# A hybrid encoder step on one core: side work timed by a model of engines and buffers instead of fixed waits

## The chip, the cores and the metric

The kernel runs on one core of a Trainium2 chip. The metric is the device time of one execution in microseconds (us); the median of three runs counts. The engines of the core are TensorE (PE: matmuls and transposes), VectorE (DVE), ScalarE (ACT), GpSimd (POOL) and SyncE (SP), which here issues the DMAs. Each has its own queue of instructions and works through it in order.

## The reference, cut to what matters

One step of a one-layer encoder over a prompt of 2048 tokens and a sample of 32, in float32, width 1024:

```python
h = rms_norm(x, norm1);  z = h @ w_in            # w_in: 1024 x 3592
qa, fa, ia, ga, qb, kb, vb, fb = split(z)
# HGRN2: 4 heads, chunks of 64 tokens, state 128 x 128 per head
f = lb + (1 - lb) * sigmoid(fa)
S_t = diag(f_t) S_{t-1} + outer(1 - f_t, ia_t);   o_t = S_t^T qa_t
oa = rms_norm(o, hgrn_out_norm) * silu(ga)
# FoX: 8 heads of 64; q and k normalized per head; c = cumsum(log_sigmoid(fb + b))
s = q @ k.T / 8 + c_q - c_k        # causal
ob = softmax(s) @ v
x = x + concat(oa, ob) @ w_out
y = x + square(relu(rms_norm(x, norm2) @ w_up)) @ w_down      # 1024 -> 4096 -> 1024
```

Normalized keys, values, the log forget values and the final states are outputs as well. The sample goes through the same weights and attends to a cache of 256 rows.

## The kernel before

The tokens are taken in four blocks of 512; block 2 carries the 32 sample tokens too (544 columns). All large products run in float32r as three matmuls: a value is split into a high part and a remainder, and `mm3` adds high by high, high by low and low by high. A strip is one weight tile against one block of tokens: 24 matmuls of 512 columns for 128 output columns and 8 slices of the inner dimension. `load_w` (L158 to L170) brings a weight tile: a DMA of 512 KB into `wr`, a cast on ACT into `wh` (L163) and four subtractions on POOL into `wl` (L169, 256 columns each). `wr`, `wh` and `wl` have two buffers each.

Dense work is these strips: the input projections of FoX (`fox`: for each of four column groups `fox_k`, `fox_v`, `fox_q`, after `fox_gate`) and of HGRN2 (`hgrn`), then `out_proj` and `ffn`. Everything else is side work. After a strip of k or q, `finish` squares the result (`squares`: a product on POOL, L290; a rounded square on ACT, L292; the difference on POOL, L294), sums the squares over a head with two matmuls into a PSUM tile `tk` or `tq`, takes the inverse root on ACT (L282, L283), scales on DVE (L427), stores, and for k transposes on PE (a second `tk`). HGRN2 does the like with `th`. `build` makes the normalized inputs of a block: for each 128 rows a DMA into `row` (L242), two squares on ACT into `junk` (L246), a root on POOL (L156), a scaling on DVE (L251) and eight transposes into two tiles `ta` (L104), each followed by a cast on ACT (L201) and a difference on DVE (L202). `attention` runs head by head over key blocks of 512; `att_max` computes row maxima (`mx`, then transposes into `mt`), `att_main` the scores `st`, the exponentials and, two steps behind, the products with the values (`ot`). Its loads `kA`, `kB`, `V` have two buffers each and are written in the code at the start of the key block that uses them.

The order in which this is emitted is set by the class `Flow` (L42 ff.). `flow.t` is a clock that each matmul advances by a modelled time. `dense` runs the generators of strips and, between matmuls, `pump` runs every side generator whose due time has come. A side generator ends a step with `yield x`: it is due again x microseconds later. These are fixed numbers: QLAT 8.0 from the squares of k and q to their sum, HLAT 7.0 for `th`, KLAT 5.0 to the transposes, BLAT 7.5 in `build`, TLAT 1.2 between the `ta` tiles, SL 4.5 after a strip, PACE for a step of attention. The framework then orders each engine's queue by its own scheduler, with the emission order as its input; the loads in particular are moved far ahead of the place where the code has them.

In time: blocks 0 and 1 of FoX until about 205 us; HGRN2 heads and FoX of blocks 2 and 3, with attention beside them, until about 1015 us; then the pools of temporaries close, the input rows of the residual are loaded (`load_x`, tiles `acc`), and `out_proj` and `ffn` run until the end, with attention beside them until about 2320 us and with `build` for each block's second norm, which reads the residual from `X`.

Of the kernel before, what the change touches and what calls it, by code (L numbers as in the profile page):

```python
# [19 lines left out]
P = 128  # L20
# [20 lines left out]
class Flow:  # L41
# [3 lines left out]
    def __init__(self):  # L45
        self.t = 0.0
        self.n = 0
        self.q = []

    def spawn(self, gen, lat=0.0):  # L50
        self.n += 1
        heapq.heappush(self.q, (self.t + lat, self.n, gen))

    def step(self):
        due, n, gen = heapq.heappop(self.q)
        self.t = max(self.t, due)
        lat = next(gen, None)
        if lat is not None:
            heapq.heappush(self.q, (self.t + lat, n, gen))
# [14 lines left out]

@with_exitstack
def hymba_step(
# [15 lines left out]
    AT = 9  # L92

    def mm(out, lhsT, rhs, start, stop):
        n = rhs.free_size()
        if rhs.dtype == F32:
            flow.t += max(n, 32) * 4 * 0.00042
        else:
            flow.t += n * 0.00042 if n >= 256 else 0.213
        pe.matmul(out, lhsT, rhs, start=start, stop=stop)  # L100

    def tp(out, in_, idn):
        flow.t += 0.109
# [13 lines left out]
    const = ctx.enter_context(tc.tile_pool(name="const", bufs=1))  # L117
    acts = ctx.enter_context(tc.tile_pool(name="acts", bufs=2))
    wpool = ctx.enter_context(tc.tile_pool(name="wpool", bufs=2))
    rows = ctx.enter_context(tc.tile_pool(name="rows", bufs=2))  # L120
    small = ctx.enter_context(tc.tile_pool(name="small", bufs=4))
    att = ctx.enter_context(tc.tile_pool(name="att", bufs=2))
    ps_x = ctx.enter_context(tc.tile_pool(name="ps_x", bufs=3, space=PSUM))
    ps_o = ctx.enter_context(tc.tile_pool(name="ps_o", bufs=1, space=PSUM))
    ps_stack = ExitStack()
    ps_mm = ps_stack.enter_context(tc.tile_pool(name="ps_mm", bufs=2, space=PSUM))
    ps_tr = ps_stack.enter_context(tc.tile_pool(name="ps_tr", bufs=2, space=PSUM))
# [14 lines left out]
    act.preload_act_table_set("natural_log_exp_and_others")  # L142
# [15 lines left out]
    def load_w(src, kt, ncols, pfx):  # L158

        raw = wpool.tile([P, kt, ncols], F32, tag="wraw", name=f"wr{pfx}", bufs=2)  # L160
        sp.dma_start(raw, src.rearrange("(k p) c -> p k c", p=P))
        hi = wpool.tile([P, kt, ncols], F32R, tag="whi", name=f"wh{pfx}")
        act.copy(hi, raw)  # L163
        lo = wpool.tile([P, kt, ncols], F32R, tag="wlo", name=f"wl{pfx}")

        fl = lambda a: a.rearrange("p k c -> p (k c)")
        for c in range(0, kt * ncols, 256):
            s = slice(c, c + 256)
            pool.tensor_tensor(fl(lo)[:, s], fl(raw)[:, s], fl(hi.bitcast(F32))[:, s], op=ALU.subtract)  # L169
# [24 lines left out]
    def to_acts(row, w, hi, lo, t0):  # L194

        for g in range(row.shape[1] // 512):
            tr = ps_tr.tile([P, 4, P], F32, tag="tr", name=f"ta{nid()}")
# [6 lines left out]
            yield TLAT  # L204
# [14 lines left out]
    def build(q, done, gb, getrow, src=None, first=False):  # L219
# [35 lines left out]
        lat = BLAT  # L255
        ts = QT[q]
        cur = prep(*ts[0])
        for i in range(len(ts)):
            nxt = prep(*ts[i + 1]) if i + 1 < len(ts) else None
            yield lat if i == 0 else lat - 3.0  # L260
# [38 lines left out]
    tmp = tmp_stack.enter_context(tc.tile_pool(name="tmp", bufs=12))  # L299
# [4 lines left out]
    def strip(col, A, qs, evac):  # L304
        hi, lo = load_w(w_in[:, col:col + P], KT, P, nid())
        for q in qs:
            ah, al = A[q]
            for c0, n in QCH[q]:
# [5 lines left out]
                if g is not None:  # L314
                    flow.spawn(g, SL)
# [5 lines left out]
    def fox_gate(A, qs):  # L321

# [5 lines left out]
        dve.tensor_tensor(w2[:, :, 32:40], wf, w2.bitcast(F32)[:, :, 0:8], op=ALU.subtract)  # L328
        for q in qs:
# [10 lines left out]
            flow.spawn(gate_tail(q, z), 2.0)  # L340

    def gate_tail(q, z):
# [30 lines left out]
            yield 6.0  # L373
# [18 lines left out]
            if nt == 5:  # L392
                sp.dma_start(nls, X[0:TS, 4, :])
                cg = small.tile([P, 2, HB], F32, tag="cg", name="cg", bufs=1)
                sp.dma_start(cg, cache_logf[0, 0].rearrange("(t p) h -> p t h", p=P))
                st = ps_tr.tile([HB, 512], F32, tag="tr", name=f"tl{nid()}")
# [13 lines left out]
    def fox_k(A, qs, s):  # L410
# [18 lines left out]
        def finish(q, z):  # L429
            n = QN[q]  # L430
            sh, sl = squares(z[:, 0:n])
            yield QLAT
# [7 lines left out]
            if n > 512:  # L440
# [893 lines left out]
    X = {}  # L1334
# [61 lines left out]
```

## Time and profile before

| | us |
|---|---|
| three runs | 2913.29, 2915.94, 2917.99 |
| median | 2915.94 |
| the profiled execution's own time | 2912.88 |
| its span in the trace | 2911.2 |
| PE busy | 2847.8 (98%) |
| DVE, ACT, POOL busy | 1680.2 (58%), 1386.3 (48%), 1278.7 (44%) |
| DMA: bytes moved, mean rate | 381.91 MB, 131 GB/s |

The busy shares are averages over stages. PE is busy nearly everywhere, so what can be gained at the same work is the sum of its gaps, and each gap has a releaser: the instruction on another engine whose end let PE go on. The granted clock of PE is 0.996 of full speed on average.

### The profile page before, as it was taken

The page shows a single profiled execution, that of the slowest core. Times are in us where ns is not written, and L with a number is a line of the kernel's source. Part 1 is how long each engine was busy: PE and PEld are TensorE (multiplying, and loading weights), DVE is VectorE, ACT ScalarE, POOL GpSimd, SP SyncE. Part 2 cuts the span into 40 slices and gives each one's busy share as a digit, 9 for nine tenths or more (in the row PEclk, how much of TensorE's full clock was granted, in tenths as well). Part 3 has the DMA queues.
Part 4 walks back from the last instruction along what each step waited for, and adds up shares of the span by engine and source line. Part 5 has one row for each costly group of instructions (what it writes and reads, how often), then busy time and mean ns, then how long its engine had stood idle before and what let it go on. Part 6 is the DMA issues. An engine that isn't in the chain of part 4 may idle for free.

```text
span 2911.2 us, 43685 instructions
## 1 busy us (share of the span) xinstructions
PE 2847.8 (98%) x15568; PEld 2423.8 (83%) x15568; DVE 1680.2 (58%) x3283; ACT 1386.3 (48%) x2447; POOL 1278.7 (44%) x1744
## 2 busy tenths in 40 slices
PE   7999999999999999999999999999999999999999
PEld 5787877988789778888888888978999989988887
DVE  6336677656666677666565555465665554443333
ACT  5555676777555545444444444444444433222222
POOL 5653344453223444444444444434333454455554
PEclk9999999999999999999999999999999999999999
DMA  6762444776324563434347344444533333243333
GB/s 180 211 170 86 122 137 127 208 193 175 87 80 116 168 227 106 123 107 122 111 123 228 117 120 116 129 134 117 180 113 102 92 109 95 87 131 105 94 94 102
DMA packets 463658, 381.91 MB, mean 131 GB/s; under 512 B 34432, under 2 KB 363408, under 8 KB 463440
## 3 DMA queue, kind: packets, MB, share of 16 engines
q1 hardware_dynamic: 463440, 379.12, 44.9%
q8 instruction: 123, 2.02, 0.3%
q14 instruction: 95, 0.78, 0.1%
HBM read 316.63 MB, written 62.40 MB: 130 GB/s over the span
## 4 chain that ended last, share of the span: by engine, by line
PE 64%; DVE 1%; ACT 0%; DMA 0%; POOL 0%; issue 0%; SPq 0%; DVEq 0%; ACTq 0%; POOLq 0%
PE mm L100 55%; PE st L100 3%; PE ot L100 3%; PE mx L100 1%; PE ta L104 0%; DMA row<-X 0%; PE rs L100 0%; DMA acc<-in_x_prompt_dram 0%; PE tx L104 0%; PE ty L104 0%; POOL wl L169 0%; DVE acc L882 0%; PE mt L104 0%; DVE pl L878 0%; ACT wh L163 0%
## 5 line engine op out<-in xcount | busy, mean ns | idle before, releaser
L169 POOL TENSOR_TENSOR wl<-wr,wh 128x256 fp32r<-128x256 f32 x1536 | 1121.2, 761 | 1500.3 <-ACT wh L163 1354.6
L100 PE MATMUL mm<-ahi,wh 128*128 128x512 f32 (+1 forms) x2528 | 895.9, 354 | 2.4 <-DVE acc L1056 1.3
L100 PE MATMUL mm<-alo,wh 128*128 128x512 f32 (+1 forms) x2528 | 881.7, 349 | 0.0
L100 PE MATMUL mm<-ahi,wl 128*128 128x512 f32 (+1 forms) x2528 | 881.2, 349 | 0.0
L163 ACT CAST wh<-wr 128x1024 fp32r<-128x1024 f32 x384 | 403.3, 1050 | 749.5 <-PE mm L100 668.4
L100 PEld LDWEIGHTS mm<-ahi,wh 128*128 128x128 f32 x2528 | 478.2, 189 | 62.3 <-DVE t L628 1.7
L100 PEld LDWEIGHTS mm<-ahi,wl 128*128 128x128 f32 x2528 | 477.2, 189 | 59.2 <-issue 0.5
L100 PEld LDWEIGHTS mm<-alo,wh 128*128 128x128 f32 x2528 | 478.4, 189 | 56.3
L1056 DVE TENSOR_TENSOR acc<-acc,mm 128x512 f32<-128x512 f32 x480 | 326.5, 685 | 161.5 <-PE mm L100 159.0
L874 ACT ACTIVATE st<-st 128x512 f32<-128x512 f32 (+1 forms) x320 | 169.3, 529 | 332.9 <-PE st L100 189.0
L878 DVE TENSOR_TENSOR pl<-st,ph 128x512 fp32r<-128x512 f32 (+1 forms) x320 | 198.5, 620 | 204.3 <-ACT ph L876 203.3
L100 PE MATMUL mm<-wh,uh 128*128 128x512 f32 x768 | 306.9, 400 | 1.3 <-ACT uh L1117 0.8
L100 PE MATMUL mm<-wh,ul 128*128 128x512 f32 x768 | 302.9, 395 | 0.0
L100 PE MATMUL mm<-wl,uh 128*128 128x512 f32 x768 | 302.8, 394 | 0.0
L1116 DVE TENSOR_TENSOR mm<-mm,r 128x512 f32<-128x512 f32 (+1 forms) x160 | 95.9, 599 | 300.6 <-ACT r L1115 299.0
L100 PEld LDWEIGHTS mm<-wh,uh 128*128 128x128 f32 x768 | 144.6, 188 | 39.3 <-DVE acc L1056 5.5
L100 PEld LDWEIGHTS mm<-wh,ul 128*128 128x128 f32 x768 | 144.9, 189 | 35.0 <-DVE ul L1118 0.2
L882 DVE TENSOR_TENSOR acc<-acc,st 128x512 f32<-128x512 f32 (+2 forms) x288 | 173.5, 602 | 0.0
L876 ACT CAST ph<-st 128x512 fp32r<-128x512 f32 (+1 forms) x320 | 169.9, 532 | 7.4
L100 PEld LDWEIGHTS mm<-wl,uh 128*128 128x128 f32 x768 | 145.0, 189 | 30.8
L834 DVE TENSOR_REDUCE mc<-mx 128x1 f32<-128x512 f32 x192 | 130.6, 686 | 41.2 <-PE mx L100 40.6
L100 PE MATMUL mm<-uh,wh 128*128 128x272 f32 x512 | 149.5, 292 | 0.2 <-DVE acc L1149 0.2
(293 smaller groups left out, 4177.6 us busy)
## 6 DMA issues: line engine op xcount, KB each, us to landing
wr<-in_w_up_dram SPq DMA_DIRECT2D x128, 512.0 KB
wr<-in_w_down_dram SPq DMA_DIRECT2D x128, 512.0 KB
wr<-in_w_in_dram SPq DMA_DIRECT2D x96, 512.0 KB
kB<-KS SPq DMA_DIRECT2D x160, 128.0 KB
kA<-KS SPq DMA_DIRECT2D x80, 256.0 KB
V<-VS SPq DMA_DIRECT2D x80, 256.0 KB
wr<-in_w_out_dram SPq DMA_DIRECT2D x32, 512.0 KB
out_dram<-t SPq DMA_DIRECT2D x32, 256.0 KB
```

What stands on the lines that cost most here:

```text
L100: pe.matmul(out, lhsT, rhs, start=start, stop=stop)
L163: act.copy(hi, raw)
L169: pool.tensor_tensor(fl(lo)[:, s], fl(raw)[:, s], fl(hi.bitcast(F32))[:, s], op=ALU.subtract)
L834: dve.tensor_reduce(out=mc[:, j, kb:kb + 1], in_=mx[:, 0:n], axis=AX.X, op=ALU.max)
L874: act.activation(st[:, off:], st[:, off:], AF.Exp)
L876: act.copy(ph[:, off:], st[:, off:])
L878: dve.tensor_tensor(pl[:, off:], st[:, off:], ph.bitcast(F32)[:, off:], op=ALU.subtract)
L882: dve.tensor_tensor(acc[:, off:], acc[:, off:], st[:, off:], op=ALU.add)
L1056: dve.tensor_tensor(acc[:, t, c], acc[:, t, c], ps, op=ALU.add)
L1116: dve.tensor_tensor(z, z, r, op=ALU.mult)
```

## The change

Side work no longer waits for a fixed time. `Flow` keeps a model: a list of busy stretches for ACT, DVE and POOL (`place` puts an instruction into the first gap in which it fits), for each tile the time at which it is ready and at which it was last used, and for each pool and tag the ring of its buffers. The engines are wrapped (`Modelled`), so that every instruction of ACT, DVE, POOL and SP enters the model with a cost by its width; the tile pools are wrapped too (`Pool`). A side generator now yields `need([tiles], (pool, tag))`, and is resumed when the model has those tiles ready and a buffer of that tag free. The matmuls of `load_w`'s tiles keep their order, and its cast and subtractions are placed on ACT and POOL as occupancy.

Besides: the `fox_gate` matmuls come after the first strip of `fox_k`, its weights before; `attention` loads a key block while the one before is worked on (`ahead`), for maxima and scores; the `ot` tile is taken at the first product with the values; PACE goes from [2.0, 2.0, 2.6, 3.5] to [0.8, 0.8, 2.6, 4.5]; the residual's tiles are named `res` instead of `acc`; a matmul of 256 columns or more counts 0.013 more on the clock. Every matmul, transpose and elementwise step is there as before, in the same shapes: 15136 matmuls in both. All instructions of ACT, DVE, POOL and SP now carry the line of the wrapper (L165), except for `load_w` (L298, L300, L306); the matmuls stand at L236 and the transposes at L241.

```diff
+    def push(self, gen, lat):
+        self.n += 1
+        cond = lat if callable(lat) else None
+        due = max(self.t, cond()) if cond else self.t + lat
+        heapq.heappush(self.q, (due, self.n, gen, cond))
...
+    def place(self, eng, r, dur):
+        iv = self.busy[eng]
...
+        for k, (x, y) in enumerate(iv):
+            if s + dur <= x:
+                i = k
+                break
+            s = max(s, y)
+        iv.insert(i, (s, s + dur))
+        return s + dur
...
+    def need(self, ins, *slots):
+        names = [self.key(a) for a in ins]
+        def when():
+            r = max([self.ready.get(n, 0.0) for n in names], default=0.0)
+            for pool, tag in slots:
+                ring, bufs = self.ring.get((pool.name, tag), ([], 1))
+                if len(ring) >= bufs:
+                    r = max(r, self.last.get(ring[-bufs], 0.0))
+            return r + 0.1
+        return when
...
+    def cost(self, name, outs, ins):
+        n = max(a.free_size() for a in (*outs, *ins))
+        if self.eng == "act":
+            return 0.07 + n * 0.001
+        if self.eng == "pool":
+            n = outs[0].free_size()
+            return 0.2 + n * (0.18 if n <= 8 else 0.0024)
...
+            if self.eng == "sp":
+                end = r + 2.3 + outs[0].nbytes() / 160e3
+            else:
+                end = fl.place(self.eng, r, self.cost(name, outs, ins)) + 0.12
...
-    KLAT, QLAT, HLAT, SL = 5.0, 8.0, 7.0, 4.5
-    BLAT, TLAT, MLAT = 7.5, 1.2, 4.0
-    PACE = [2.0, 2.0, 2.6, 3.5]
+    act, dve, pool, sp = (Modelled(flow, n, e) for n, e in (("act", act), ("dve", dve), ("pool", pool), ("sp", sp)))
+    MLAT = 4.0
+    PACE = [0.8, 0.8, 2.6, 4.5]
...
+        flow.place("act", flow.t, 0.07 + kt * ncols * 0.001)
+        flow.place("pool", flow.t, kt * ncols * 0.003)
...
         for g in range(row.shape[1] // 512):
+            yield need([row], (ps_tr, "tr"))
             tr = ps_tr.tile([P, 4, P], F32, tag="tr", name=f"ta{nid()}")
...
             sh, sl = squares(z[:, 0:n])
-            yield QLAT
+            yield need([sh, sl], (ps_tr, "tr"))
             norm(z[:, 0:512], sh[:, 0:512], sl[:, 0:512])
...
-        yield from fox_gate(A, qs)
+        w2 = gate_weights()
         for s in range(4):
             yield from fox_k(A, qs, s)
+            if s == 0:
+                yield from fox_gate(A, qs, w2)
...
+    def ahead(load, units):
+        seq = [(h, kb) for h, qb in units for kb in range(qb + 1)]
+        nxt = load(*seq[0])
+        for k in seq[1:] + [None]:
+            cur, nxt = nxt, None if k is None else load(*k)
+            yield cur
...
-            kB = att_load_kb(h, kb, 1)
-            kA = att.tile([P, 512], F32R, tag="kA", name=f"kA{nid()}")
...
-            if kb == 0:
-                yield 3.0
+            kB, kA, V = next(kvs)
...
+                yield need([qA, qC, kA, kB, V, *(pvs[0].ins if len(pvs) == LAG else ())], (ps_x, "x"),
+                           *([(ps_o, "ot")] if kt == LAG else []))
```

What stands in the queues, at three places. First POOL's queue while FoX of block 0 runs. `wl` are `load_w`'s subtractions; the rows on `t` are the two steps of `squares`. Before:

```order
L169 TENSOR_TENSOR wl104_694<-wr104_690,wh104_692 128x256 x4
L169 TENSOR_TENSOR wl119_788<-wr119_784,wh119_786 128x256 x4
L169 TENSOR_TENSOR wl127_838<-wr127_834,wh127_836 128x256 x4
L290 TENSOR_TENSOR t123_823<-t118_782 128x512
L294 TENSOR_TENSOR t125_827<-t123_823,t124_825 128x512
L169 TENSOR_TENSOR wl133_880<-wr133_876,wh133_878 128x256 x3
L290 TENSOR_TENSOR t129_865<-t126_832 128x512
L169 TENSOR_TENSOR wl133_880<-wr133_876,wh133_878 128x256
L294 TENSOR_TENSOR t131_869<-t129_865,t130_867 128x512
```

After, at the same stage:

```order
L306 TENSOR_TENSOR wl100_651<-wr100_647,wh100_649 128x256 x4
L165 TENSOR_TENSOR t90_592<-t89_590 128x512
L165 TENSOR_TENSOR t92_596<-t90_592,t91_594 128x512
L306 TENSOR_TENSOR wl111_729<-wr111_725,wh111_727 128x256 x3
L165 TENSOR_TENSOR t97_641<-t96_639 128x512
L306 TENSOR_TENSOR wl111_729<-wr111_725,wh111_727 128x256
L165 TENSOR_TENSOR t99_645<-t97_641,t98_643 128x512
```

Over the whole program there are 48 such pairs. In 14 places of before a subtraction of `wl` stands inside a pair, and in 33 of after. The matmuls that PE's queue has between the end of the strip and the sum of its squares went from 65 to 122 (k and q, 32 pairs) to 17 to 75, in most of them 23 to 27; for `th` (16 pairs) from 35 to 64 to 22 to 100.

Second, ACT's queue where `build(2)` has a row's squares among FoX of block 1 (`row704` before, `row717` after; `tk` and `tq` are the roots of the norms, `mm` the copies of strips). Before:

```order
L163 CAST wh152_1000<-wr152_998 128x1024
L530 CAST t141_933<-tv138_921 128x4x64
L476 COPY t142_940<-mm134_885 128x512
L246 ACTIVATE junk706_3947,ss705_3946<-row704_3944 128x512
L282 ACTIVATE tk145_961<-tk145_961,epsc_241 128x512
L246 ACTIVATE junk707_3949,ss705_3946<-row704_3944 128x512
L283 ACTIVATE tk145_961<-tk145_961 128x512
```

After:

```order
L165 COPY t156_1018<-mm152_979 128x512
L165 ACTIVATE t158_1022<-t156_1018 128x512
L165 ACTIVATE junk719_3994,ss718_3993<-row717_3991 128x512
L165 ACTIVATE junk720_3996,ss718_3993<-row717_3991 128x512
L165 COPY t162_1060<-mm161_1035 128x512
L165 ACTIVATE tk163_1062<-tk163_1062,epsc_241 128x512
L300 CAST wh180_1150<-wr180_1148 128x1024
```

In both the row of the later block stands ahead of the norm `tk` of the block that PE works on. Third, SP's queue at the start of `out_proj` (`acc` or `res`: the input rows of the residual, 256 KB each; `wr`: weights of `w_out`). Before:

```order
L161 DMA wr_11758<-in_w_out_dram 128x2x512
L1043 DMA acc_11548<-in_x_prompt_dram 128x512 x8
L1043 DMA acc_11570<-in_x_prompt_dram 128x512 x6
L274 DMA alo_11573<-MTL 128x2x512
L161 DMA wr_11816<-in_w_out_dram 128x2x512
```

After:

```order
L165 DMA res_11855<-in_x_prompt_dram 128x512 x8
L165 DMA res_11877<-in_x_prompt_dram 128x512 x4
L165 DMA kB_275<-KS 64x512
L165 DMA kB_275<-NC 2x512
L165 DMA kA_12007<-KS 128x512
L165 DMA V_12009<-VS 128x4x128
L165 DMA kB_266<-NC 2x512
L165 DMA MTH<-mh_12056 128x512
L165 DMA MTL<-ml_12058 128x512
L165 DMA res_11877<-in_x_prompt_dram 128x512
L165 DMA ahi_11879<-MTH 128x2x512
L165 DMA wr_12099<-in_w_out_dram 128x2x512
```

The first `wr` of before is the fourth of `w_out`, and four stand ahead of the rows; of after two stand ahead of them, and the `wr` shown is the third.

## Rows read from the trace of the kernel before

**Rows 1.** The page, part 1: busy us, share of the span, instructions.

```profile
PE 2847.8 (98%) x15568; PEld 2423.8 (83%) x15568; DVE 1680.2 (58%) x3283; ACT 1386.3 (48%) x2447; POOL 1278.7 (44%) x1744
```

**Rows 2.** Windows by stage: length, busy us by engine, PE clock, DMA share, GB/s.

```profile
30.00:1010.00 980.00, 948.58 (x5579) 800.41 (x5578) 600.42 (x1306) 611.96 (x1204) 421.22 (x508) 0.99 0.52 146
1010.00:1040.00 30.00, 26.46 (x105) 18.81 (x104) 25.60 (x50) 16.31 (x31) 8.54 (x12) 1.00 0.86 292
...
1890.00:1930.00 40.00, 35.17 (x168) 28.05 (x168) 27.59 (x49) 21.37 (x41) 16.45 (x27) 0.97 0.52 155
```

**Rows 3.** Waits of PE, 30 to 1012 us: total us, times, longest.

```profile
PE mt L104 <- DVE t L756: 4.2, 1, 4.2
PE tk L104 <- DVE t L427: 4.0, 1, 4.0
PE th L100 <- POOL t L294: 3.3, 1, 3.3
...
PE xa L100 <- DVE AT L660: 0.2, 1, 0.2
```

**Rows 4.** Windows in which the granted clock is about half.

```profile
97.70:104.60 6.90, 4.82 (x14) 3.99 (x15) 3.10 (x3) 4.19 (x10) 6.61 (x7) 0.51 0.54 157
445.80:452.80 7.00, 5.68 (x20) 4.41 (x21) 5.28 (x15) 2.53 (x5) 0.00 (x0) 0.51 0.65 191
...
991.90:995.50 3.60, 3.60 (x11) 2.79 (x10) 0.92 (x2) 1.93 (x4) 0.00 (x0) 0.53 0.49 146
```

**Rows 5.** Timeline near 94 us: start, duration, operation, in brackets idle before and releaser.

```profile
86.81 0.64 SPq L242 DMA_DIRECT2D row<-in_x_prompt_dram  x1
...
94.57 0.63 ACT L246 ACTIVATE junk<-row 128x512 bf16<-128x512 f32 x1 [4.71 <-DMA row<-in_x_prompt_dram]
...
97.69 1.29 DVE L251 SCALAR_TENSOR_TENSOR row<-row,rs,gbc 128x1024 f32<-128x1024 f32 x1 [7.87 <-POOL rs L156]
...
95.18 0.39 PE L100 MATMUL mm<-alo,wh 128*128 128x512 f32 x1
95.40 0.39 PE L100 MATMUL mm<-ahi,wl 128*128 128x512 f32 x1
99.78 1.09 PE L104 MATMUL tk<-identr,t 128*128 128x128 f32 x4 [3.99 <-DVE t L427]
```

**Rows 6.** POOL's operations by line (shortest/median/longest ns), and the timeline near 987 us.

```profile
L169 POOL TENSOR_TENSOR wl<-wr,wh x1536: 716/738/1830, 24.5 to 2898.0; 128x256 fp32r<-128x256 f32 x192
...
L290 POOL TENSOR_TENSOR t<-t x48: 1030/1043/2012, 37.8 to 1011.7; 128x512 f32<-128x512 f32 x36, 128x544 f32<-128x544 f32 x12
...
L294 POOL TENSOR_TENSOR t<-t,t x48: 1257/1297/1753, 41.6 to 1012.8; 128x512 fp32r<-128x512 f32 x36, 128x544 fp32r<-128x544 f32 x12
...
986.55 3.18 POOL L169 TENSOR_TENSOR wl<-wr,wh 128x256 fp32r<-128x256 f32 x3
...
986.80 1.22 DVE L635 TENSOR_TENSOR t<-t,he 128x512 f32<-128x512 f32 x1
...
991.00 0.50 PE L100 MATMUL th<-t,oner 128*128 128x512 f32 x1 [3.32 <-POOL t L294]
```

**Rows 7.** Timeline at the start of `out_proj`: SP's issues and a cast of ACT.

```profile
1026.91 0.45 SPq L161 DMA_DIRECT2D wr<-in_w_out_dram  x1
1027.51 9.94 SPq L1043 DMA_DIRECT2D acc<-in_x_prompt_dram  x14
...
1036.47 1.05 ACT L163 CAST wh<-wr 128x1024 fp32r<-128x1024 f32 x1 [2.77 <-issue]
```

**Rows 8.** Timeline of ACT at two other rows of `build`.

```profile
438.79 0.63 ACT L246 ACTIVATE junk<-row 128x512 bf16<-128x512 f32 x1 [2.87 <-DMA row<-in_x_prompt_dram]
...
1919.58 0.63 ACT L246 ACTIVATE junk<-row 32x512 bf16<-32x512 f32 x1 [5.55 <-DMA row<-X]
```

**Rows 9.** Operations on the key tile `kA`: count, ns, first and last start.

```profile
L100 PE MATMUL st<-qA,kA x320: 277/392/479, 222.8 to 2322.5; 128*128 128x512 f32 x128, 128*128 128x256 f32 x32
L856 SPq DMA_DIRECT2D kA<-KS x80: 319/344/809, 63.7 to 2282.4; - x80
```

More of the change, by code (lines that the diff above doesn't have):

```diff
@@ new lines, in after, with done @@
+    def after(self, outs, ins, part=False):
+        r = self.t
+        for a in ins:
+            r = max(r, self.ready.get(self.key(a), 0.0))
+        for a in outs:
+            if not part:
+                r = max(r, self.last.get(self.key(a), 0.0))
+            if a.name in self.pred:
+                r = max(r, self.last.get(self.pred.pop(a.name), 0.0))
+        return r
+    def done(self, outs, ins, end):
+        for a in outs:
+            self.ready[self.key(a)] = max(self.ready.get(self.key(a), 0.0), end)
+        for a in (*outs, *ins):
+            self.last[self.key(a)] = max(self.last.get(self.key(a), 0.0), end)
@@ L96, in mm @@
         if rhs.dtype == F32:
-            flow.t += max(n, 32) * 4 * 0.00042
+            cost = max(n, 32) * 4 * 0.00042
         else:
-            flow.t += n * 0.00042 if n >= 256 else 0.213
+            cost = n * 0.00042 + 0.013 if n >= 256 else 0.213
+        flow.last[out.name] = 0.0
+        product(cost, out, lhsT, rhs)
         pe.matmul(out, lhsT, rhs, start=start, stop=stop)
     def tp(out, in_, idn):
-        flow.t += 0.109
+        flow.last[out.name] = 0.0
+        product(0.109, out, in_)
         pe.transpose(out, in_, idn)
@@ L253, in prep @@
             return row, w, t0
-        lat = BLAT
         ts = QT[q]
@@ L935, in attention @@
         qA, qC, mpad = att_load_q(h, qb)
-        yield 3.0
-        for _ in att_max(h, qb, qC, mpad):
-            yield 0.6
+        kbs = ahead(lambda h, kb: att_load_kb(h, kb, 0), units)
+        kvs = ahead(att_load_kv, units)
+        yield from (x for x in att_max(h, qb, qC, mpad, kbs) if x is not None)
         for i, (h, qb) in enumerate(units):
@@ L941, in attention @@
             nx = None
+            steps, have = 0, 0
             if i + 1 < len(units):
@@ L951, in attention @@
                 while nx is not None and have < steps * m // (tot + 1):
-                    have += 1
-                    if next(nx, -1) is None:
-                        yield 0.3
+                    x = next(nx, -1)
+                    if callable(x):
+                        yield x
+                    else:
+                        have += 1
+                        if x == -1:
+                            break
                 yield lat / 2
             if nx is not None:
-                for _ in nx:
-                    yield 0.6
+                for x in nx:
+                    if x is not None:
+                        yield x
                 qA, qC, mpad = n
```

210 lines of the change are left out of this document (142 added, 68 removed).

## The prediction, made before the changed kernel ran

> **What bounds the kernel now.** I read the page's first part, then the windows by stage, then PE's waits, then the timeline around the longest of them. PE is busy for 2847.8 of 2911.2 us [rows 1], and the change leaves every matmul in place. So nothing but the gaps can be won, and the windows tell where they lie: 980 - 948.6 = 31.4 us from 30 to 1010 us, 3.5 at the transition to `out_proj`, 4.8 around 1910 us [rows 2]. The rest is the start, on which the change has no hold, and crumbs in the FFN.
>
> Two things make a gap dearer than it looks. A matmul lasts 0.39 us but the next starts after 0.22 to 0.23 [rows 5], so a gap that the trace counts from the end of the last one has already cost 0.16 more. And after a long gap the granted clock falls to about half, the lower of its two levels (1.2 against 2.4 GHz): five windows show 0.51 to 0.53, two of 4.82 and 5.68 us of PE work and three of 3.60 [rows 4]. At half clock that work costs 4.82 x 0.49 = 2.4, 2.8 and three times 1.7 us. Each of these windows follows one of the longest gaps.
>
> What ends the gaps: 28 waits in the stretch to 1012 us, of which the three longest are 4.2 (`mt`), 4.0 (`tk`) and 3.3 us (`th`) [rows 3]. The timeline of the 4.0 shows a pattern. The row of the next block's `build` was issued at 86.81 and landed only for ACT's square at 94.57, after 4.71 us in which ACT stood at that instruction. The norm of `tk` stands behind it in ACT's queue, and on DVE the scaling of the row (L251) stands ahead of `tk`'s (L427) for 7.87 us more; PE waits 3.99 us for that [rows 5]. So a transfer of a later block held a chain that PE needed now. The `mt` wait at 447 us has the same head: ACT stood 2.87 us at a row [rows 8]. The wait around 1920 us too: a row from `X`, 5.55 us [rows 8]. The `th` wait is another: three chunks of `wl` (3.18 us) stand between the two POOL steps of a square [rows 6].
>
> **The change part by part.** I cost it against the profiled execution (2912.9 us, 3.0 below the median of the runs) and add the difference to the median.
>
> *A, rows of `build` ahead of ACT's queue.* Two waits, 4.2 + 4.0 us, 2 x 0.16 hidden, 2.4 + 2.8 of clock: 13.7 us. The model gives a load 2.3 us plus its bytes, and the row of 512 KB about 5.6 by that; the row at 86.81 took 7.8 [rows 5]. The model's rule holds the transposes back until the row is ready, but it does not hold back the square, which is emitted when `build` runs. In the changed order ACT still has the row's squares ahead of `tk`'s roots. I counted the matmuls that PE has between the DMA's issue and the last ACT instruction ahead of the square, for 12 such rows, at 0.23 us each: before 0.0 to 8.4 us (9 of 12 at 3.0 or less), after 0.0 to 7.0 (5 of 12). For the row of the 4.0 us wait it is 6.4 before and 5.9 after. So one of the two waits is to be expected again: half goes, **-6.9**.
>
> *B, the other side waits to 1010 us.* 31.4 - 4.2 - 4.0 - 3.3 = 19.9 us in 25 waits, 25 x 0.16 = 4.0 hidden, 1.7 of clock: 25.6. They are handoffs, a result of ACT or DVE that PE's queue met too early: the fixed waits were too short there, or another side step came between. The new conditions ask for the tile itself and a free buffer. Walking back through the changed queues, the worst shortfalls between what a tile needs and the PE work ahead of its use become smaller in nearly every family. Against it: side steps that are due together now stand together; stretches of side work of more than 1.6 us without a strip's matmul go from 24 (52 us) to 42 (96 us). In the trace of before such stretches ran without gaps but for the transition, so I price them at nothing; they have the running side instructions as cover, and if that is gone, each can show a handoff. Two thirds go: **-17.1**.
>
> *C, POOL's squares.* The `th` wait goes: 3.3 + 0.16 + 1.7 = 5.2. New ones come. The chain from the strip's end to the sum is 0.16 + 0.63 (ACT's copy) + 1.04 + 1.30 (POOL) + some 0.1 for each of three handoffs (estimated from the 0.05 between L294's end and the matmul at 991.00) = 3.4 us [rows 5, 6]; each chunk of `wl` inside the pair adds 0.74. Before, some 14 us of PE work covered it for k and q; after, 23 matmuls, 5.3 us, in most. With no or one chunk it holds, with three (3.4 + 2.2 = 5.6) it doesn't. Chain by chain 5 of 48 fall short, by 0.3 to 1.5 us, together some 5. **0** in sum, and the cover is the point to watch.
>
> *D, the row from `X`.* 4.8 us [rows 2] in 3 waits, 0.5 hidden, 1.7 of clock: 7.0. In the changed order that row has 2.7 us of PE work between issue and square instead of none, and the residual's loads stand behind it. Two thirds go: **-4.7**.
>
> *E, the transition.* SP needs 9.94 us to issue 14 row loads, and the weights issued ahead of them at 1026.91 were cast at 1036.47 [rows 7], 9.6 us later. Now the third `w_out` tile stands behind 12 of them (8.5 us). Two strips of 24 matmuls, 11 us, precede its use, one of which has run when the loads are issued. The upper bound is 8.5 + 9.6 - 5.5 = 12.6 us of new gap, the lower none (the row loads may be let go earlier, since their buffers set that); I take the middle, **+6**, as no row shows the case.
>
> *Loads one block ahead, gate, PACE.* No wait of PE is put down to a key or value load, and the first `kA` is issued at 63.7 us for a use at 222.8 [rows 9]: the scheduler already lifts these loads as far as two buffers allow, and there are still two. Zero; if a load were late it would show as a wait of `st`. The gate's 16 matmuls moved behind the first strip cover the same thing on either side. PACE packs the early attention and ends it sooner; PE's work is the same. Zero.
>
> Sum: -6.9 - 17.1 + 0 - 4.7 + 6 = -22.7; 2915.9 - 22.7 = **2893**.
>
> **The rivals.** *Slower: POOL is the wait that takes the place of the ones removed.* The model holds the sum of squares back for POOL's work at a fixed price, but POOL's real times spread: L290 up to 2.01, L294 to 1.75, a chunk to 1.83 us [rows 6]. With the longest pair and one long chunk the chain is 0.16 + 0.63 + 2.01 + 1.75 + 0.3 + 1.83 = 6.7, with medians and three chunks as at 986.55 (3.18) it is 6.6: 1.3 us over the cover of 5.3. If that were the mean over the 32 chains of k and q it would give 32 x 1.3 = 42 us: 2893 + 42 = **2935**. It decides from a mean shortfall of 0.9 us per chain (29 us, the gain and the bound of 5.8 together). For it: 33 chunks inside the pairs instead of 14, and a fixed price that knows no spread. Against: the medians lie at the low end, and half the chains have no chunk inside.
>
> The chunks at 986.55 were 1.06 us each beside a DVE product of two tiles in SBUF (986.80), against a median of 0.74 [rows 6]. The Trainium skill ("SBUF — State Buffer", Who interferes with whom) says that a DVE instruction with two SBUF inputs contends with a GpSimd instruction that reads SBUF, over a shared port; the trace agrees here. The model prices POOL without it. If all 33 chunks were stretched so, that is 33 x 0.32 = 10.6 us, and the sum by it would be 2904.
>
> *The waits only move.* Rows of a later block still stand in ACT's queue, and denser side work finds other late handoffs: A and B give a quarter instead, some 10 us, and E takes 6 back: 2916 - 4 = **2912**, between 2906 and 2920. For it: the pattern of A is untouched in kind.
>
> *Nearly all goes.* A to D whole, C's new waits and E at nothing: 13.7 + 25.6 + 5.2 + 7.0 = 51 less: **2865**. Against: the row pattern.
>
> *The change doesn't do what it says:* loading ahead does nothing, since the scheduler does it already. That is in the sum at zero.
>
> **How the numbers follow.** About 0.2% (5.8 us) is what a measurement here can tell from no change. Forecast (2877 to 2906) 0.45; nearly all goes 0.12; waits only move 0.23, two thirds of it within 5.8 us of the median; slower by POOL 0.20. Faster 0.45 + 0.12 + 0.08 = 0.65, same 0.15, slower 0.20. The range leaves out the lower part of the case in which nearly all goes and the upper half of the slower one: 2862 to 2926. With A and B whole or at a quarter, C between -5 and +10 and E between 0 and 12.6 the sum itself spans 2867 to 2924, inside it.
>
> **What would show it.** Right: PE's waits from 30 to 1010 us add to some 12 to 18 us instead of 31; `tk` or `mt` still once behind a `junk<-row`; the `th` wait on L294 gone, but `tq` and `tk` now with waits on POOL of about 1 us; a gap of `mm` on `wl` or `wh` shortly after `out_proj` starts. Wrong: waits on POOL at most k and q chains (the slower rival); a sum over 25 (moved only); `st` on a DMA of `kA`, `kB` or `V` (loading ahead does matter). What would break the sum is a new wait of a kind that before does not have, above all in the FFN, where before has nearly none.

## The result, and the profile after

The changed kernel is slower: 2958.37 us median of four runs (2955.86 to 2961.22) against 2915.97 for the kernel before; the ratio is 1.0146, with a 95% interval from 1.0129 to 1.0164. Forecast were 2893 us and a range from 2862 to 2926. The time lies outside it, on the other side of the old one. The profiled execution, the longest of the four, took 2961.2 us, with a span of 2959.5, 48.3 us more than that of before.

The page's first part, the line that answers to [rows 1]:

```profile
PE 2874.5 (97%) x15568; PEld 2432.5 (82%) x15568; DVE 1684.4 (57%) x3283; ACT 1386.6 (47%) x2447; POOL 1275.9 (43%) x1744
```

The matmuls are the same (the traces of both count 15568 with the transposes; the 15136 named with the change stand in neither) and DVE, ACT and POOL do the same work to within 5 us. PE is idle for 85.0 us (2959.5 - 2874.5) instead of 63.4, and "busy" for 26.7 us longer with the same matmuls. Windows as in [rows 2] (length, busy us of PE, PEld, DVE, ACT, POOL, then PE's granted clock, DMA share, GB/s):

```profile
30.00:1010.00 980.00, 933.00 (x5377) 778.53 (x5377) 596.50 (x1294) 601.12 (x1185) 395.23 (x481) 0.98 0.51 141
1010.00:1040.00 30.00, 28.67 (x165) 23.39 (x164) 21.62 (x47) 16.46 (x31) 9.19 (x12) 1.00 0.72 203
1040.00:1300.00 260.00, 247.24 (x1126) 196.42 (x1127) 200.31 (x360) 137.33 (x243) 103.51 (x148) 0.98 0.50 148
...
1900.00:2300.00 400.00, 398.84 (x2476) 359.75 (x2475) 209.51 (x399) 166.26 (x283) 175.34 (x253) 1.00 0.43 126
```

From 30 to 1010 us PE is idle for 47.0 us (31.4 before), from 1010 to 1300 for 14.1. From 1900 to 2300 it is 1.2, where before had 4.8 around 1910 alone.

The same clock time is not the same work. The last sum of HGRN2's norms (`th`) starts at 1015.5 us before and at 1077.3 now, and the first matmul of `out_proj` a few us behind it (1021.3 and 1080.9). Cut there, the stretches are, for before and then for the changed kernel:

```profile
30.00:1016.00 986.00, 954.58 (x5606) 805.31 (x5604) 605.01 (x1313) 615.52 (x1210) 424.55 (x511) 0.99 0.52 146
1016.00:1300.00 284.00, 279.14 (x1257) 225.78 (x1256) 196.00 (x342) 131.97 (x223) 126.48 (x184) 1.00 0.47 143
```

```profile
30.00:1078.00 1048.00, 995.67 (x5713) 828.61 (x5713) 645.41 (x1388) 640.61 (x1255) 421.45 (x513) 0.98 0.51 142
1078.00:1300.00 222.00, 213.24 (x955) 169.73 (x954) 173.02 (x310) 114.31 (x203) 86.48 (x128) 0.98 0.52 153
```

So up to the end of HGRN2 PE is idle for 52.3 us instead of 31.4, and from there to 1300 us for 8.8 instead of 4.9.

The waits that make it, rows of PE's waits over the whole span (us in all, times, longest; the start's are left out):

```profile
PE tq L236 <- POOL t L165: 14.4, 15, 1.9
...
PE tk L236 <- POOL t L165: 9.7, 10, 2.5
...
PE ot L236 <- ACT ph L165: 4.4, 6, 1.7
PE st L236 <- DVE acc L165: 3.9, 3, 2.5
PE st L236 <- ACT qC L165: 3.3, 2, 2.5
PE th L241 <- DVE t L165: 3.3, 1, 3.3
```

The first two rows are new: 25 waits of the sums of squares of k and q on POOL, 24.1 us. Before had one of 0.8. The half-clock windows have become ten instead of five. Three of them (columns as above):

```profile
40.90:44.30 3.40, 3.40 (x9) 2.63 (x9) 2.04 (x3) 1.41 (x3) 0.00 (x0) 0.52 0.39 72
126.20:129.60 3.40, 3.40 (x9) 1.87 (x10) 0.41 (x1) 2.19 (x3) 1.38 (x3) 0.52 0.52 140
...
1075.20:1082.00 6.80, 6.40 (x16) 4.55 (x16) 5.57 (x14) 3.23 (x7) 2.02 (x2) 0.50 0.84 276
```

All ten hold 43.5 us of PE work, about half of it lost: 21 us, against 10 in the five of [rows 4]. That is 11 of the 48.3 us; idle time is 21.6 more. The other 15 or so are in "busy" at the full clock: each wait hides 0.16 us in the end of the matmul ahead, and some 65 more matmuls start 0.1 to 0.2 us late without any gap that the view lists (counted from the start-to-start times of all matmuls against the usual one of their kind).

What a new wait looks like. The timeline of ACT, POOL and PE from 98 us on:

```profile
98.02 1.06 ACT L300 CAST wh<-wr 128x1024 fp32r<-128x1024 f32 x1 [1.31 <-PE mm L236]
98.97 0.58 ACT L165 COPY t<-mm 128x512 f32<-128x512 f32 x1
...
99.15 2.13 POOL L306 TENSOR_TENSOR wl<-wr,wh 128x256 fp32r<-128x256 f32 x3 [4.97 <-ACT wh L300]
101.22 1.06 POOL L165 TENSOR_TENSOR t<-t 128x512 f32<-128x512 f32 x1
102.22 0.76 POOL L306 TENSOR_TENSOR wl<-wr,wh 128x256 fp32r<-128x256 f32 x1
102.92 1.29 POOL L165 TENSOR_TENSOR t<-t,t 128x512 fp32r<-128x512 f32 x1
...
104.26 0.50 PE L236 MATMUL tq<-t,two 128*128 128x512 f32 x1 [1.05 <-POOL t L165]
```

The end of a strip releases two things nearly at once: the strip's result, which ACT copies for the squares, and the buffer `wh`, into which ACT casts the next weight. The cast goes first (98.02), the copy follows at 98.97, and of the cast's four chunks three stand on POOL ahead of the square and one inside the pair. So the difference of the squares ends at 104.2, 6.2 us after the cast began, and PE stands for 1.05 us. The same order comes back strip after strip: 1.05 us for `tq` at 104, 173, 193 and 214 us. For `tk` at 91, 112, 160, 180 and 201 us it is 0.61 to 0.63, with all four chunks ahead of the square and none inside the pair. At each of the 25 waits three or four chunks stand directly ahead of the square or inside the pair; at 21 of them none or one is inside.

The kernel before has this order too. Here three chunks stand ahead and one inside, as above, but the two sums come 8.2 us after the difference has ended:

```profile
143.66 2.14 POOL L169 TENSOR_TENSOR wl<-wr,wh 128x256 fp32r<-128x256 f32 x3 [0.81 <-ACT wh L163]
145.74 1.06 POOL L290 TENSOR_TENSOR t<-t 128x512 f32<-128x512 f32 x1
146.74 0.76 POOL L169 TENSOR_TENSOR wl<-wr,wh 128x256 fp32r<-128x256 f32 x1
147.44 1.31 POOL L294 TENSOR_TENSOR t<-t,t 128x512 fp32r<-128x512 f32 x1
...
156.93 0.63 PE L100 MATMUL tk<-t,two 128*128 128x512 f32 x2
```

### The profile page after: what moved, and what is told of

It reads as the page before. It is cut to its first block, busy times and chain, and to the rows that moved or that the text cites. A ratio compares the mean times of both kernels' runs of the same rounds, so it can differ in the third digit from the quotient of the medians.

```text
span 2959.5 us, 43753 instructions
## 1 busy us (share of the span) xinstructions
PE 2874.5 (97%) x15568; PEld 2432.5 (82%) x15568; DVE 1684.4 (57%) x3283; ACT 1386.6 (47%) x2447; POOL 1275.9 (43%) x1744
## 4 chain that ended last, share of the span: by engine, by line
PE 71%; DVE 1%; ACT 1%; POOL 1%; issue 1%; DMA 1%; SPq 0%; ACTq 0%; DVEq 0%; POOLq 0%
PE mm L236 59%; PE st L236 3%; PE ot L236 3%; PE mx L236 2%; POOL wl L306 1%; DVE t L165 0%; PE xo L236 0%; PE ta L241 0%; PE xu L236 0%; PE xa L236 0%; PE th L241 0%; PE rs L236 0%; ACT wh L300 0%; ACT t L165 0%; PE tx L241 0%
## 5 line engine op out<-in xcount | busy, mean ns | idle before, releaser
L306 POOL TENSOR_TENSOR wl<-wr,wh 128x256 fp32r<-128x256 f32 x1536 | 1120.7, 761 | 1536.9 <-ACT wh L300 1445.4
L236 PE MATMUL mm<-ahi,wh 128*128 128x512 f32 (+1 forms) x2528 | 897.6, 355 | 1.1 <-DVE t L165 1.1
L236 PE MATMUL mm<-alo,wh 128*128 128x512 f32 (+1 forms) x2528 | 883.6, 350 | 1.1 <-DVE alo L165 1.1
L236 PE MATMUL mm<-ahi,wl 128*128 128x512 f32 (+1 forms) x2528 | 883.4, 349 | 0.0
L300 ACT CAST wh<-wr 128x1024 fp32r<-128x1024 f32 x384 | 404.1, 1052 | 833.6 <-PE mm L236 761.3
L165 DVE TENSOR_TENSOR res<-res,mm 128x512 f32<-128x512 f32 (+1 forms) x720 | 431.5, 602 | 257.5 <-PE mm L236 254.0
L236 PEld LDWEIGHTS mm<-ahi,wh 128*128 128x128 f32 x2528 | 480.4, 190 | 62.6 <-issue 2.3
L236 PEld LDWEIGHTS mm<-alo,wh 128*128 128x128 f32 x2528 | 480.9, 190 | 58.5 <-DVE alo L165 2.0
L236 PEld LDWEIGHTS mm<-ahi,wl 128*128 128x128 f32 x2528 | 479.6, 190 | 59.4 <-POOL wl L306 0.4
L236 PE MATMUL mm<-wh,uh 128*128 128x512 f32 x768 | 306.8, 399 | 1.1 <-ACT uh L165 0.8
L165 ACT ACTIVATE st<-st 128x512 f32<-128x512 f32 (+1 forms) x320 | 169.5, 530 | 287.4 <-PE st L236 155.2
L236 PE MATMUL mm<-wl,uh 128*128 128x512 f32 x768 | 302.0, 393 | 0.0
L236 PE MATMUL mm<-wh,ul 128*128 128x512 f32 x768 | 301.6, 393 | 0.0
L165 DVE TENSOR_TENSOR pl<-st,ph 128x512 fp32r<-128x512 f32 (+1 forms) x320 | 198.6, 621 | 167.0 <-ACT ph L165 165.2
L165 DVE TENSOR_TENSOR mm<-mm,r 128x512 f32<-128x512 f32 (+1 forms) x160 | 95.8, 598 | 334.0 <-ACT r L165 332.0
L236 PEld LDWEIGHTS mm<-wh,uh 128*128 128x128 f32 x768 | 144.4, 188 | 40.6 <-DVE res L165 6.8
L165 ACT CAST ph<-st 128x512 fp32r<-128x512 f32 (+1 forms) x320 | 170.4, 532 | 7.5 <-DMA MTH<-mh 0.5
L165 DVE TENSOR_TENSOR acc<-acc,st 128x512 f32<-128x512 f32 (+2 forms) x288 | 173.6, 603 | 0.0
L236 PEld LDWEIGHTS mm<-wh,ul 128*128 128x128 f32 x768 | 144.5, 188 | 34.7 <-DVE ul L165 0.2
L236 PEld LDWEIGHTS mm<-wl,uh 128*128 128x128 f32 x768 | 144.5, 188 | 31.2
L165 DVE TENSOR_REDUCE mc<-mx 128x1 f32<-128x512 f32 x192 | 130.1, 685 | 48.5 <-PE mx L236 48.2
L236 PE MATMUL mm<-uh,wh 128*128 128x272 f32 x512 | 150.1, 293 | 0.4 <-DVE res L165 0.4
```

Source lines behind the costliest of these rows:

```text
L165: f(*args, **kw)
L300: raw_act.copy(hi, raw)
L306: raw_pool.tensor_tensor(fl(lo)[:, s], fl(raw)[:, s], fl(hi.bitcast(F32))[:, s], op=ALU.subtract)
```

## Experiments

All kernels were timed beside the kernel before on the same chip. Where nothing else is said, the ratio to it is given with its 95% interval; the changed kernel's is 1.0146 [1.0129, 1.0164].

**The distance alone, on the kernel before.** One number is changed:

```diff
-    KLAT, QLAT, HLAT, SL = 5.0, 8.0, 7.0, 4.5
+    KLAT, QLAT, HLAT, SL = 5.0, 0.5, 7.0, 4.5
```

> The kernel before, with one number changed: QLAT 0.5 instead of 8.0, so that the sum of the squares of k and q stands about as close behind the squares as in the changed kernel. Theory S (that distance alone makes the new waits, whatever else the change does): waits of tk and tq on POOL at most of the 32 chains, 20 to 30 us in all, and 2936 to 2948 instead of 2916. Rival (it needs the changed order of the other engines too): under 2925.

Measured: 2935.25 us, 1.0063 [1.0048, 1.0078], 19 us more than before. PE's waits from 30 to 1010 us:

```profile
PE tq L100 <- POOL t L294: 8.9, 11, 3.1
PE tk L100 <- POOL t L294: 7.1, 9, 1.9
...
PE tk L100 <- ACT t L292: 3.5, 3, 2.9
```

The same waits come at the same matmuls, 20 of them with 16.0 us on POOL (19.5 with those on ACT), a microsecond short of the forecast span in the time. So bringing the sum close to the squares is enough for the new waits. Not all of the 19 us need be theirs: the framework reordered the rest, and the waits of `mx` on `mc` (L834) grew from 1.9 to 7.0 us.

**The distance alone, undone in the changed kernel.**

```diff
             sh, sl = squares(z[:, 0:n])
+            yield 8.0
             yield need([sh, sl], (ps_tr, "tr"))
```

> The changed kernel, but in the norms of k and q 8 us are let pass between the squares and the model's condition for their sum. Theory S (the sum of squares comes too early: POOL has the chunks of the next weight ahead of the square and inside the pair, the model does not see them there): the 25 waits of tk and tq on POOL (24.1 us, 29 with what the end of a matmul hides) and the two half-clock windows that follow the longest of them (3.4 us) go, 2926 to 2933 instead of 2958. Rival theory M (the gaps only move, since dense side work finds a late handoff wherever it is put): the tk and tq waits go, others of like sum come, 2948 or more.

Measured: 2946.68 us (2940.01 to 2951.22), 1.0101 [1.0082, 1.0120]: 12 us less, not 25 to 32. The waits of `tq` are gone and those of `tk` are down to 3.4 us, but others have grown (`tk`'s transposes, `tl`, `xu`, `tv`, `mm` on `wl`). Neither theory's number was met: less than half of the gain stays. These waits are read from the profiled execution, at 2940.0 us the shortest of the four; its mean granted clock was 0.995, that of the other three 0.992.

**The model's own error.** The model places the next weight's cast and chunks when the next strip begins, after the squares of the strip just ended were placed. Here they are placed at the strip's end, ahead of them; `load_w` places nothing for these strips:

```diff
+                if q == qs[-1] and c0 + n == QN[q]:
+                    end = flow.place("act", flow.t, 1.09)
+                    flow.place("pool", end, 3.07)
                 g = evac(q, c0, n, ps)
```

> The changed kernel; in the model alone the cast and the four POOL chunks of the next weight are placed at the end of a strip, ahead of the squares, instead of behind them at the next strip's start. Theory S in its exact form (the model sees POOL free when the next weight's chunks have it): most of the 25 waits of tk and tq on POOL go, 2928 to 2940 instead of 2958. Rival (the model's placing does not matter, the costs of single steps are too low): still more than 15 such waits, 2950 or more.

Measured: 2946.18 us, 1.0102 [1.0085, 1.0119]. Of the 25 waits of `tq` and `tk` on POOL one is left, of 2.0 us; instead:

```profile
PE th L236 <- POOL t L165: 7.4, 3, 3.4
PE th L236 <- ACT t L165: 5.3, 2, 4.7
PE mx L236 <- DVE acc L165: 4.5, 1, 4.5
```

So the model's error was the one that the timeline shows: with the cast and the chunks placed where they are on the chip, it lets the sum come late enough. But the time fell by 12 us and not by 18 to 30, so that neither span was met: HGRN2's `th` took over, and the clock was lower, with a mean of 0.989 to 0.990 in the four runs against 0.992 to 0.994 in the changed kernel's. Two ways of removing nearly all of the same waits gave the same 12 us.

How close the sums stand behind the squares can be counted in each trace, over the 32 chains of k and q. Slack is the time from the end of the difference on POOL to the start of the matmul that reads it; a chunk is directly ahead if less than 0.2 us of idle time lies between:

| kernel | squares with chunks directly ahead | pairs with a chunk inside | median slack, us | waits of `tk` and `tq` on POOL |
|---|---|---|---|---|
| before | 28 | 9 | 6.7 | 1, 0.8 us |
| changed | 27 | 17 | 0.05 | 25, 24.1 us |
| before, QLAT 0.5 | 27 | 3 | 0.05 | 20, 16.0 us |
| changed, 8 us let pass | 16 | 16 | 3.2 | 4, 3.4 us |
| changed, chunks placed first | 25 | 23 | 2.5 | 1, 2.0 us |

The waits go with the slack and not with the chunks inside the pairs: three pairs with one go with 20 waits, 23 with a single one.

**More room for every condition.**

```diff
-            return r + 0.1
+            return r + 1.5
```

> The changed kernel with 1.5 us instead of 0.1 added to every condition of the model. If the conditions are right in kind and only tight by about a us (theories S and, for the other handoffs, the like), all tq and tk waits but one or two go, and most other waits under 1.5: 2915 to 2930. If the order itself is at fault (theory M or P): 2945 to 2960.

Measured: 2920.79 us (ten runs), 1.0011 [1.0001, 1.0020]: 38 us of the 42 are back with one constant, inside the span forecast for conditions that are only too tight. Five waits of `tk` and `tq` on POOL stay, not one or two. PE's waits over the whole span:

```profile
PE st L236 <- DVE mc L165: 5.3, 6, 1.9
...
PE tk L236 <- POOL t L165: 3.8, 2, 2.5
...
PE tq L236 <- POOL t L165: 2.7, 3, 1.6
```

**Where that room counts.** The 1.5 us on the three sums of squares alone, then on all other conditions, then on the five conditions of attention:

```diff
-    def need(self, ins, *slots):
+    def need(self, ins, *slots, m=0.1):
...
-            yield need([sh, sl], (ps_tr, "tr"))
+            yield need([sh, sl], (ps_tr, "tr"), m=1.5)
```

> The changed kernel with 1.5 us added to the conditions of the three sums of squares alone (tk, tq, th). The margin everywhere gave 2921, 38 less. If squares are the greater part of that (theory S): most of the tk and tq waits go and the time is 2930 to 2940. If the rest of the handoffs carries it (theory L: every condition was tight, and each handoff by itself costs little): 2943 to 2955.

Measured: 2939.06 us, 1.0082 [1.0067, 1.0097], 19 us less than the changed kernel. Three of the 25 waits are left (4.4 us); a new one of 9.2 us, of `tv` on DVE, stands beside them.

> The changed kernel with 1.5 us added to all conditions but those of the three sums of squares. Theory S: the 25 waits on POOL stay (some 24 us), 2938 to 2950. Theory L: 2925 to 2935, with waits on POOL still there but fewer others. With the run beside it the two parts should add up to about 38 us; if they add up to far less, the parts help each other.

Measured: 2945.65 us (2937.15 to 2947.96), 1.0108 [1.0091, 1.0124], 13 us less; the waits on POOL are still there, and longer (the profiled execution is the shortest of the four):

```profile
PE tq L236 <- POOL t L165: 18.5, 13, 3.2
PE tk L236 <- POOL t L165: 12.0, 11, 2.4
```

> The changed kernel with 1.5 us added to the five conditions of attention alone (maxima, scores, products with the values, the sum at the end). The margin on all but the squares gave 13 us. If it is attention's handoffs, packed around 440 to 560 and 1040 to 1100 us (theory P with tight conditions): 2942 to 2950. If it is the handoffs of HGRN2, FoX and build: within 4 us of 2958.

Measured: 2952.79 us, 1.0126 [1.0109, 1.0143]: 6 us less, between the two spans, and the intervals overlap, so that attention's share is not established. 19 + 13 = 32 of the 38: the parts nearly add up, and squares are the greater one.

**Pace.**

```diff
-    PACE = [0.8, 0.8, 2.6, 4.5]
+    PACE = [2.0, 2.0, 2.6, 3.5]
```

> The changed kernel with the old PACE [2.0, 2.0, 2.6, 3.5]. Theory P (the faster pace of the early attention packs side work into stretches without strips, which gives the waits and the four half-clock windows between 440 and 552 us, some 21 us more than before there): 2938 to 2946, and no half-clock window in that stretch but at most one. Rival (the conditions on tiles make those stretches, PACE does not): within 4 us of 2958.

Measured: 2951.69 us, 1.0128 [1.0110, 1.0145]. 7 us less, between the two spans, and the intervals overlap. From 440 to 560 us two half-clock windows of 3.4 us are left of four with 23.8, but PE is idle there for 8.3 us against 10.6. The pace is at most a small part. The old pace together with the margin on the squares gave no time, so whether the two add up was not measured.

**Loading ahead, taken out of the changed kernel and put into the one before.**

```diff
-        nxt = load(*seq[0])
-        for k in seq[1:] + [None]:
-            cur, nxt = nxt, None if k is None else load(*k)
-            yield cur
+        for k in seq:
+            yield load(*k)
```

> The changed kernel with key blocks loaded at the block that uses them. Prediction's step: the scheduler already lifts these loads, so 2955 to 2962. Rival (loading ahead moves DMAs and matmuls at the transition and makes the waits of st and mx there): 2945 or less. Second rival (it helps): 2965 or more.

> The kernel before with key blocks loaded one block ahead and nothing else of the change. In the changed kernel undoing it cost 6 us. Prediction's step (the scheduler lifts the loads anyway): within 5 us of 2916. Rival (it is a gain of its own): 2906 to 2911.

Measured: 2964.30 us, 1.0164 [1.0148, 1.0179], without it; 2918.00, 1.0009 [1.0000, 1.0018], in the kernel before. Taking it out cost 6 us, between the step's span and the second rival's, with overlapping intervals, and no wait of PE in its trace is put down to a key or value load. The end of attention, of which two windows stand here, fell into a stretch with few strips (25 and 23 matmuls in 10 us, where the changed kernel has 82 and 81):

```profile
2350.00:2360.00 10.00, 7.83 (x25) 3.85 (x23) 8.21 (x14) 5.60 (x10) 0.00 (x0) 1.00 0.56 165
2360.00:2370.00 10.00, 8.66 (x23) 4.58 (x23) 8.53 (x17) 4.00 (x8) 0.00 (x0) 0.83 0.30 85
```

Put into the kernel before it gained nothing.

**Rows of `build` held back.** The squares of a row wait for the model to have it loaded:

```diff
+            if not first:
+                yield need([row])
             ss = small.tile([P, 2], F32, tag="ss", name=f"ss{nid()}")
```

> The changed kernel; in build the squares of a row are held until the model has the row loaded, instead of being emitted with its DMA. Step A of the prediction (a row that has not landed holds ACT, and the wait at 441 us in the changed kernel has that head): the waits of ACT on rows from 30 to 1010 us fall from 12 us to under 5, the wait of 3.3 us and its half-clock window (3.4 us) go: 2945 to 2953. Rival (other side steps are late there anyway): within 4 us of 2958.

> The changed kernel with 1.5 us added to every condition and with the squares of a row held until it is loaded. If both act for themselves, the 2921 of the margin alone less 5 to 12: 2909 to 2916, level with the kernel before or a little under it. If rows are not what is left: 2918 to 2924.

Measured: 2951.32 us, 1.0122 [1.0107, 1.0137], alone; 2936.41, 1.0065 [1.0050, 1.0080], with the 1.5 us on all conditions. Alone, the time lies in the span forecast for step A, but by luck: its sign, fewer waits of ACT on rows, did not come, and the wait of PE that they head is still there (`th`, 3.5 us). Three of the four runs had a mean granted clock of 0.995 against 0.992 to 0.994, which by the estimate at the end of the next section can account for some 4 of the 7 us. The second misses both spans. ACT still stands at rows, here in the first of the two from 30 to 1010 us:

```profile
ACT junk L165 <- DMA row<-in_x_prompt_dram: 12.7, 6, 5.3
```

12.7 us against 12.2 in the changed kernel: holding the square in the emission did not put it behind the landing in ACT's queue. Together with the margin it is 16 us slower than the margin alone. One new wait is 6.8 us of a `tq` on ACT; no run tells why the order fell so.

**More room in the kernel before.**

```diff
-    KLAT, QLAT, HLAT, SL = 5.0, 8.0, 7.0, 4.5
-    BLAT, TLAT, MLAT = 7.5, 1.2, 4.0
+    KLAT, QLAT, HLAT, SL = 7.0, 8.0, 9.0, 4.5
+    BLAT, TLAT, MLAT = 9.5, 1.2, 4.0
```

> The kernel before with three fixed waits longer by 2 us: KLAT 7, HLAT 9, BLAT 9.5. Theory L (slack between a step and its use costs nothing while there are strips to run, and what is late costs PE time): the waits on th and rows shrink, 2905 to 2914. Rival (before has slack enough, its remaining gaps are of another kind): 2912 to 2922.

Measured: 2921.01 us, 1.0019 [1.0009, 1.0028], if anything slower. The `th` wait on POOL and the two that rows headed are gone, but others have grown in their place: PE is idle for 67.2 us, against 63.4 before. So the theory that room is free and only lateness costs is too simple; another order came out, with gaps of its own. No kernel was shown to be faster than the one before; the margin of 1.5 us comes to within 5 us of it.

## Why the prediction was wrong, point by point

*What bounds the kernel* held: PE's work did not change, and the time is in gaps and clock.

*Step C failed first.* "With no or one chunk it holds" was counted from the chunks inside the pair, and 21 of the 25 waits have none or one there. The cast and the chunks ahead of the square, which start at the same strip's end, were left out: 0.95 us on ACT and 2.07 us on POOL (99.15 to 101.22) in the timeline above. With them the chain is 3.4 + 0.7 + 0.95 + some 1.5 (2.07 less the copy's 0.58, beside which the first chunks run), 6.5 us, against a cover of 5.3: short by 1.2, as PE shows with 1.05. The trace of before had shown it: there 28 of 32 squares stand behind chunks, hidden by 6.7 us of slack. The term was not 0 but +20 of idle time (24.1 less the 4.1 of before on POOL) and, with the hidden ends and the clock, some 25. The shortening of QLAT in the kernel before gave 19 us by itself. The slower rival had the place, and nearly the price (1.3 us in each of 32 chains; it was 0.6 to 1.1 in most of 25), but mostly for another reason: it laid the price on long POOL times, and the steps in the timeline have their median ones (1.06, 1.29, chunks of 0.71 and 0.76). Over all 25 chains what the steps took beyond their medians adds up to some 5 us.

The Trainium skill's rule on the shared port ("SBUF — State Buffer", Who interferes with whom) had been weighed there. The chain at 98 us does not need it: DVE was idle, and the chunks were not stretched. The longest wait of `tq`, 1.89 us at 126.09, agrees with that rule: three chunks inside the pair took 3.10 us, where three take 2.13 in the timeline above, beside a DVE instruction that reads two tiles. That instruction is the scaling of a row of `build`, so that a row had a part in this wait as well:

```profile
120.79 2.05 DVE L165 SCALAR_TENSOR_TENSOR row<-row,rs,gbc 128x1024 f32<-128x1024 f32 x1 [1.88 <-POOL rs L165]
121.72 3.10 POOL L306 TENSOR_TENSOR wl<-wr,wh 128x256 fp32r<-128x256 f32 x3
...
126.09 0.60 PE L236 MATMUL tq<-t,two 128*128 128x512 f32 x1 [1.89 <-POOL t L165]
```

*Step B failed as well.* Up to the end of HGRN2 the gaps other than those on POOL were 31.4 - 3.3 - 0.8 = 27.3 us before and are 52.3 - 24.1 = 28.2 now. The prediction had taken 24 us, A and B with their hidden ends and clock, out of this; nothing of it came. The sentence that failed is "two thirds go": it took the model's ready times for the chip's. That a condition met to within 0.1 us in the model is often met late on the chip is argued, not shown wait by wait. The margin fits it: 1.5 us on the conditions other than squares gave 13 us back, and in its trace the waits after the first 30 us that are not on POOL fell from 48 (39.9 us) to 35 (29.0).

*Step A held in kind.* One of the two row waits was to come again, and it did:

```profile
436.98 0.63 ACT L165 ACTIVATE junk<-row 128x512 bf16<-128x512 f32 x1 [3.22 <-DMA row<-in_x_prompt_dram]
...
439.68 1.28 DVE L165 SCALAR_TENSOR_TENSOR row<-row,rs,gbc 128x1024 f32<-128x1024 f32 x1 [4.50 <-POOL rs L165]
440.88 0.68 DVE L165 TENSOR_TENSOR t<-t,th 128x512 f32<-128x512 f32 x1
...
441.62 1.12 PE L241 MATMUL th<-identr,t 128*128 128x128 f32 x4 [3.29 <-DVE t L165]
```

It is the chain of [rows 5] again: a row that ACT stands at, the row's scaling on DVE ahead of a norm's, and PE for 3.29 us. The other, the `tk` at 99 us, is gone as expected. One reading in the prediction was wrong: DVE's 7.87 us ahead of the row are idle time that overlaps ACT's 4.71, not time on top of it.

*Step D held*: the wait on the row from `X` went (1.2 us idle from 1900 to 2300, no half-clock window there).

*Step E had the size and not the cause.* Idle from the end of HGRN2 to 1300 us went from 4.9 to 8.8, +4 where +6 was put, with some 3 us of half clock on top. But it is not the `w_out` tile behind the rows, which is the fourth and not the third: three were issued ahead of the rows, at 1046.55, 1053.84 and 1066.38 us, the next at 1102.86. The predicted gap of `mm` on `wl` came, and is 1.8 us in all. Most waits are attention's, where it runs among few strips; the first two of these three fall before the end of HGRN2:

```profile
1042.11 0.50 PE L236 MATMUL st<-qC,kB 98*128 98x512 f32 x1 [2.52 <-DVE acc L165]
...
1074.38 0.51 PE L236 MATMUL ot<-ph,V 128*128 128x512 f32 x1 [1.72 <-ACT ph L165]
...
1091.96 0.47 PE L236 MATMUL mx<-kB,qC 96*128 96x512 f32 x1 [1.36 <-DMA res<-in_x_prompt_dram]
```

For the third the profile names a load of `res`; the matmul reads `kB` and `qC`, and a load of `qC` was issued at 1086.35, just ahead of the rows, so which load held it is not settled. The stretches of side work without strips, priced at nothing in step B, are where these stand.

*Loading ahead at zero* held for the kernel before (1.0009). *The clock* was priced only as it stood: the old windows with the gaps expected to go. The new gaps brought new windows, 11 us more.

In sum, from the two profiled executions: C about +25 instead of 0; A and B about +9, nearly all of it clock, instead of -24; D about -6 instead of -4.7; E about +7 with its clock instead of +6. The remaining 13 or so of the 48 are for the most part the matmuls that start late without a listed gap, for which the prediction had no term. The range failed because its bounds were worked out term by term from the gaps that were there, with C's upper end at +10; the rival had the larger price, and with 20% it stood for 2935, since the gain of the other steps was left in it.

What stays open: why removing the squares' waits gives 12 us by one edit (twice) and 19 by another. The clock is a part of it. Between the two profiled executions a mean clock lower by 0.004 came with 11 us of lost work, some 3 us for each 0.001; by that estimate the run with the chunks placed first lost 6 us more than the one with the margin on the squares (0.990 against 0.992). For the run with 8 us let pass it explains nothing. The framework's scheduler reorders every queue after each edit, so that each edit also moved waits that it was not aimed at, by amounts that no run separates. Nor is it settled how much of the other 20 us is attention's: its own margin and its pace gave 6 and 7 us, both with intervals that overlap the changed kernel's.

## What to carry to other kernels

When a wait is shortened to "as soon as ready", walk the whole chain on each engine from the common release, with the work that the same release starts ahead of it, and not only the steps of the chain itself: here the end of a strip started the next weight's cast and chunks too. A chain that never made anyone wait can still be long: read its slack in the trace of before, not only its waits. A condition from a model of engines needs a margin of the size of that model's error; 1.5 us of it was worth 38 us here. And where a new order makes new gaps, price the clock for those as well, not only for the gaps that go.

## What had not been expected of the hardware

Half clock came after single waits of less than 2.5 us. In the changed kernel windows at a granted clock of 0.50 to 0.52, the lower of its two levels, follow single waits of 2.45 (39.5 us), 1.89 (126.1 us) and 1.72 us (1074.4 us), where [rows 4] had windows that followed waits of 3.3 us and more besides one of 1.9. Not each such gap is followed by one: after the 2.52 us at 1042.1 the clock stays at 1.00.
